# Making the weights' lower parts by an adding DMA instead of a subtraction

## The chip, the core and the metric

The kernel runs on one core of a Trainium2 chip. The metric is the time of one execution on the device, in microseconds; several executions are timed and their median is given. The core has five engines with instruction queues of their own: TensorE (PE in the profile; its weight loads are PEld), VectorE (DVE), ScalarE (ACT), GpSimd (POOL) and SyncE (SP), and 16 DMA engines that all queues share.

## What is computed

The reference is a decoder trunk of two layers on 512 tokens of 1024 features, in float32. Every layer has four sub-layers, each with a norm before and after it and a residual:

```python
for l in range(DEPTH):
    h = rmsnorm(x, ff1_pre_g[l])
    x = x + 0.5 * rmsnorm(swiglu(h, ff1_w1[l], ff1_w3[l], ff1_w2[l]), ff1_post_g[l])
    h = rmsnorm(x, mix_pre_g[l])
    y = token_mixer(h, ...)              # pooling, sparse attention and gMLP branches, gated and merged
    x = x + rmsnorm(y, mix_post_g[l])
    h = rmsnorm(x, mem_pre_g[l])
    y = memory_cross_attention(h, ...)   # 4 heads, into 256 memory tokens
    x = x + rmsnorm(y, mem_post_g[l])
    h = rmsnorm(x, ff2_pre_g[l])
    x = x + 0.5 * rmsnorm(swiglu(h, ff2_w1[l], ff2_w3[l], ff2_w2[l]), ff2_post_g[l])
```

## The kernel before

Products of float32 operands are made on TensorE in the format float32r, which holds fewer bits. So every operand is split into two parts, an upper part (the operand rounded to float32r) and a lower part (the operand less its upper part), and one product becomes three: upper times upper, upper times lower, lower times upper (`mm3`, line 439).

The weights come in blocks of 128 x 1024 values, 512 KB each, in the order of their use (`plan`). `Weights` (line 308) leads a block through three stations. `pump` issues its load on SP's queue into one of three raw buffers (`raw`, line 328). `parts` (line 348) splits it into one of four split buffers (`wh`, an upper and a lower half): ScalarE copies the raw block into the upper half (`act`, the instruction is at line 394), then `lo` has VectorE (line 398) or GpSimd (line 413) subtract the upper half from the raw block, whichever the planner takes to be done sooner, with the bonus `spare`. After that the raw buffer is free for a later load, which waits for it in SP's queue. `next` hands a block to the products (line 429), and `release` frees its split buffer after them. `ahead` says how many blocks ahead of the one in use may be split: 2, and 4 in the output products of a sub-layer. Some blocks aren't split (the compression's `cw1`, `wst`, `poolw`); they stay in a raw buffer until TensorE has used them.

There are 482 loads and 462 splits. A feed-forward layer has 66 blocks, of which 44 are used one after the other for 24 products of 512 columns each. Places in which the blocks' order differs:

- `first_blocks`: a sub-layer starts with four blocks on the first 256 tokens (24 products of 256 columns each), then, when the norm and transposition of the other tokens are done, the same four blocks on the other 256. Seven sub-layers start so behind another one.
- `token_out`: the output products of a sub-layer. Its last four blocks are used together, tile of tokens by tile of tokens (four tiles, six products of each block for a tile), so that the norm of the first tile can begin while the others are multiplied. There are eight of these. The next sub-layer's tokens are normed tile by tile by `chain` and `pre_norm` on VectorE, ScalarE and, for the power -1/2, GpSimd (line 468), then transposed on TensorE (line 437).
- The mixer's start: unsplit compression blocks (16 short products each) alternate with projection blocks.
- The cross-attention: 8 key blocks with 24 products of 256 columns, then 8 value blocks with 12 products of 512 columns, with the attention's own products between the later ones.

The program's order is made by a planner, `Clock`: a discrete estimate of when each engine is free and when each operand is ready, by which every helper (`act`, `tt`, `gtt`, ...) puts its instruction into the program. On the chip every engine runs its queue in that order and waits for semaphores.

Of the kernel before, what the change touches and what calls it, by code (L numbers as in the profile page):

```python
# [167 lines left out]
class Slots:  # L168
    """Buffers, each with the time from which it is free."""

# [18 lines left out]
    def retire(self, tiles):  # L189
        """These are given out no more."""  # L190
        self.gone = tiles
        self.free = [x for x in self.free if not any(x[2] is e for e in tiles)]
# [9 lines left out]
class Clock:  # L202
    """The order of the program: what the engines beside the tensor engine do is put into it where its operands are
    about ready, by an estimate of what every instruction takes."""

# [47 lines left out]
    def wait(self, when):  # L253
        """The main line's: time passes."""
        assert not self.inside
        while self.heap and self.heap[0][0] <= when:
            self.step()
        self.pe = self.now = max(self.pe, when)
# [10 lines left out]
    def reach(self, key):  # L269
        """The main line's wait for an event."""  # L270
        n = 0
        while key not in self.events:
            self.step()
            n += 1
            assert n < 100000, key
        self.wait(self.events[key])

    def after(self, *keys, margin=0.0):
        """A task's wait for events."""
        for key in keys:  # L280
            while key not in self.events:
                yield self.now + 0.2
            if self.events[key] + margin > self.now:
                yield self.events[key] + margin

    def take(self, slots, keep=0):
        """A task's wait for a buffer, of which `keep` others must be left."""
        while len(slots.free) <= keep or slots.first() > self.now:
            yield self.now + 0.2 if len(slots.free) <= keep else slots.first()
        return slots.pop()[2]  # L290

    def get(self, slots):
        """The main line's wait for a buffer."""
        n = 0
        while not slots.free:
            self.step()
            n += 1
            assert n < 100000
        when, _, t = slots.pop()
        self.wait(when)  # L300
        return t
# [6 lines left out]
class Weights:  # L308
    """The weights in the order of their use: loaded ahead, and split into two parts ahead."""

# [37 lines left out]
    def parts(self, k):  # L348
        b, n = self.b, k.cols
        raw, hi, lo = k.raw[:, :n], k.hl[:, 0, :n], k.hl[:, 1, :n]  # L350
        yield b.act(hi, raw, AF.Copy)
        r = b.lo(lo, raw, hi)
        self.raws.put(r, k.raw)
        k.raw = None
        k.ready = r
        self.pump()
# [28 lines left out]
class Builder:  # L385
    def __init__(self, tc, d, out):
        self.tc, self.nc, self.d, self.out = tc, tc.nc, d, out
        self.ck = Clock()
        self.spare = -0.5

    # Instructions, each with an estimate of the time at which its result is there.

# [22 lines left out]

    def lo(self, out, src, hi):
        """A block of weights' lower part, by whichever engine has it sooner."""
        ck = self.ck
        n = size(out)
        v = max(ck.free["v"], ck.now) + 0.07 + 0.00105 * n  # L420
        g = max(ck.free["g"], ck.now) + 0.1 + 0.0024 * n
        if g < v + self.spare:
            return self.gtt(out, src, hi.bitcast(F32), OP.subtract)
        return self.tt(out, src, hi.bitcast(F32), OP.subtract)

    def mm(self, out, w, x, first, last):
# [13 lines left out]
    def mm3(self, out, w, x, first, last):  # L440
        """out += w.T @ x for float32 operands given as their two exact parts."""
        (wh, wl), (xh, xl) = w, x
        self.mm(out, wh, xh, first, False)
        self.mm(out, wh, xl, False, False)
        self.mm(out, wl, xh, False, last)

    def split(self, hi, lo, src, scale=None, bias=None):
        """hi + lo = src, a tensor on chip, each with float32r's bits. To be run by a task; returns the time."""
        if scale is not None:
# [8 lines left out]
    def row(self, dst, src_row, n, eng=None):  # L458
        """A row of DRAM to every partition."""
        (eng or self.nc.gpsimd).dma_start(dst, bass.AP(tensor=src_row.tensor, offset=src_row.offset, ap=[[0, 128], [1, n]]))  # L460
        self.ck.op("g", 1.0)

    def rstd(self, out, ss, a, b):
        """out = (ss * a + b) ** -0.5. To be run by a task; returns the time."""
        n = out.shape[-1]
        v = self.small.tile([128, 4], F32, name="v", bufs=8)
        yield self.ts(v[:, :n], ss, float(a), float(b), OP.mult, OP.add)
        self.nc.gpsimd.tensor_tensor(out, v[:, :n], self.neghalf[:, :n], OP.pow)  # L468
        return self.ck.op("g", 0.46)
# [76 lines left out]
    def pre_norm(self, m, at, ng, left):  # L546
        """Normalises a tile of tokens from the sums of squares and transposes it, for sub-layer `at`."""
        ck = self.ck
# [28 lines left out]
    def proj(self, blk, bank, n0=0, n1=S):  # L577
        """bank[feature, token] = block.T @ h, over the whole of the contraction."""
        for k in range(KD):
# [10 lines left out]
    def first_blocks(self, keys):  # L590
        """The first products of a sub-layer, on the first half of the tokens while the others get ready."""
        ck = self.ck
# [7 lines left out]
        for m in (2, 3):  # L600
            ck.reach(("T", self.at, m))
        self.spare = -0.5
        for blk, bank in got:
# [4 lines left out]
    def token_out(self, l, ph, name, lhs, ready, nk, scale, tail):  # L608
        """y[token, :] = lhs.T @ w, its norm, the residual, and the next sub-layer's norm."""
        nc, ck, ws = self.nc, self.ck, self.ws  # L610
# [71 lines left out]
        blks = []  # L682
        self.spare = 4.0
        for m in range(NT):
# [48 lines left out]
    def gelu(self, out, z2, zh, t, scale):  # L733
        """out = zh (1 + tanh(c (z + a z^3))), with z2 = z^2, zh a multiple of z and the scale to match."""
        yield self.stt(t, z2, 1.0 / GA, zh, OP.add, OP.mult)
# [3 lines left out]
    def mixer(self, l, ph):  # L739
        tc, nc, d, ck = self.tc, self.nc, self.d, self.ck  # L740
        F, H, PS, ws, at = self.f, self.hl, self.ps, self.ws, self.at
        with tc.tile_pool(name=f"mix{l}", bufs=1) as pool, tc.tile_pool(name=f"mixs{l}", bufs=1) as few:
# [71 lines left out]

            # The keys, the queries and the compressed branch's tokens.
            KS = [ck.get(H), ck.get(H)]
# [18 lines left out]
            def blocks_of(s):  # L835
                """The overlapping blocks with their positions, two tokens to a column of partitions."""
                out = []
# [13 lines left out]
            def keys_evac(bank, i, dst, key):  # L851
                """Both halves of the partitions hold a group's keys."""
                r = 0.0
# [12 lines left out]
            def queries(c, bank):  # L866
                """Over the partitions: a head's upper and lower parts, in either order."""
                q = yield from ck.take(H)
# [20 lines left out]

            # The compression, beside the gMLP's projections.  # L890
            U, hid = [None] * 4, {}
# [14 lines left out]
            def hidden(s):  # L906
                """gelu of the hidden features, [feature, (half, group, block)], and the second product."""
                F.put(ck.now, *B[s])
# [51 lines left out]
            def gated_values(m, bank):  # L960
                """gelu and layer norm of a tile of tokens; doubling its input only scales the norm's epsilon."""
                yield from ck.after(("row", at, "gm"))
# [39 lines left out]

            self.spare = 2.5
            compress(1, 0)
# [45 lines left out]

            # The gMLP's products over the tokens.
            GM = [None] * 4
# [75 lines left out]
            def spatial():  # L1128
# [9 lines left out]
                F.put(ck.now, *VG, wst, rows["lng"], rows["lnb"], rows["gm"])  # L1138
                self.spare = -0.5

            tasks = self.attention(few, dict(KS=KS, KW=KW, V=V, VC=VC, Q=Q, gates=gates, msel=msel, mwin=mwin,
# [3 lines left out]

            # The pooling mixer.
            PL = [None] * 4
# [61 lines left out]
    def attention(self, few, o):  # L1209
        """The three branches of the sparse attention; returns its tasks."""  # L1210
        nc, ck = self.nc, self.ck
# [68 lines left out]
        def spreader():  # L1280
            """The probabilities of a block of keys, [key, token], in two parts."""
            for n in range(8):
# [55 lines left out]
        def output(n, bank):  # L1338
            """The values' two parts lie in the two halves of the partitions."""
            c, g = divmod(n, 2)  # L1340
# [234 lines left out]
```

## Time and profile before

| what | value |
|---|---|
| median of 3 runs | 2781.05 us (2778.61 to 2781.05) |
| span of the profiled execution | 2778.1 us |
| TensorE busy | 2728.2 us (98%) |
| VectorE busy | 1418.9 us (51%) |
| ScalarE busy | 1038.0 us (37%) |
| GpSimd busy | 324.3 us (12%) |
| DMA moved | 270.45 MB, mean 97 GB/s |
| TensorE's granted clock, mean | 0.996 |

The profiled execution is another one than the timed ones; its span runs from its first to its last instruction and lies 2.95 us under the median. In a row of the timeline the columns are the start and the duration in us, the engine, the line in the kernel, the operation, the tiles written and read (buffer numbers left out) and their shape, how many instructions the row merges, and in brackets the engine's idle time before the row and what ended it. In a row of a group the columns are line, engine, operation, tiles, shape, count, and then busy time in us and mean ns of one, idle time before them, and what ended most of it.

### The profile page before, as it was taken

The page shows a single profiled execution, that of the slowest core. Times are in us where ns is not written, and L with a number is a line of the kernel's source. Part 1 is how long each engine was busy: PE and PEld are TensorE (multiplying, and loading weights), DVE is VectorE, ACT ScalarE, POOL GpSimd, SP SyncE. Part 2 cuts the span into 40 slices and gives each one's busy share as a digit, 9 for nine tenths or more (in the row PEclk, how much of TensorE's full clock was granted, in tenths as well). Part 3 has the DMA queues.
Part 4 walks back from the last instruction along what each step waited for, and adds up shares of the span by engine and source line. Part 5 has one row for each costly group of instructions (what it writes and reads, how often), then busy time and mean ns, then how long its engine had stood idle before and what let it go on. Part 6 is the DMA issues. An engine that isn't in the chain of part 4 may idle for free.

```text
span 2778.1 us, 34462 instructions
## 1 busy us (share of the span) xinstructions
PE 2728.2 (98%) x13624; PEld 2303.3 (83%) x13624; DVE 1418.9 (51%) x2536; ACT 1038.0 (37%) x1894; POOL 324.3 (12%) x299
## 2 busy tenths in 40 slices
PE   8999999999999999999999999999999999999998
PEld 7888888887888888888888888888778898888887
DVE  4443254889536554442354432639885465544422
ACT  3222234456435443222232222445564354432221
POOL 0000020411222020000010000213112220200000
PEclk9999999999999999999999999999999999999999
DMA  4232224311234323332233322342122343233322
GB/s 144 94 112 98 99 89 125 101 58 61 84 114 123 113 77 99 114 99 97 78 99 105 107 93 97 88 135 87 54 69 84 106 143 104 70 101 107 99 93 74
DMA packets 77970, 270.45 MB, mean 97 GB/s; under 512 B 10160, under 2 KB 10672, under 8 KB 77808
## 3 DMA queue, kind: packets, MB, share of 16 engines
q1 hardware_dynamic: 71568, 255.56, 28.6%
q0 software_dynamic: 3136, 10.25, 1.4%
q10 hardware_dynamic: 3104, 2.45, 0.3%
q8 instruction: 106, 1.74, 0.3%
q14 instruction: 56, 0.46, 0.0%
HBM read 266.12 MB, written 2.10 MB: 97 GB/s over the span
## 4 chain that ended last, share of the span: by engine, by line
PE 89%; DVE 8%; ACT 1%; issue 1%; DMA 0%; POOL 0%; ACTq 0%; SPq 0%; DVEq 0%; POOLq 0%
PE ps L429 86%; PE ps L437 2%; DVE x L402 2%; DVE hl L398 1%; DVE wh L398 1%; DVE f L407 1%; DVE ast L398 1%; ACT junk L394 1%; DVE f L1224 0%; DVE f L402 0%; DVE f L398 0%; DVE mf L1224 0%; DVE mf L407 0%; DVE sty L398 0%; DMA raw<-in_ff_w_dram 0%
## 5 line engine op out<-in xcount | busy, mean ns | idle before, releaser
L429 PE MATMUL ps<-hh,wh 128*128 128x512 f32 (+1 forms) x4864 | 1402.5, 370 | 1.8 <-ACT hh L394 1.4
L429 PEld LDWEIGHTS ps<-hh,wh 128*128 128x128 f32 x4864 | 886.6, 190 | 149.4 <-ACT hh L394 1.8
L429 PE MATMUL ps<-hlo,wh 128*128 128x512 f32 (+1 forms) x2432 | 899.6, 370 | 0.1
L398 DVE TENSOR_TENSOR wh<-raw,wh 128x1024 fp32r<-128x1024 f32 x402 | 505.9, 1261 | 604.6 <-ACT wh L394 604.1
L394 ACT ACTIVATE wh<-raw 128x1024 fp32r<-128x1024 f32 x462 | 485.1, 1052 | 729.6 <-PE ps L429 437.0
L429 PEld LDWEIGHTS ps<-hlo,wh 128*128 128x128 f32 x2432 | 462.3, 190 | 72.5 <-DVE v L409 0.4
L429 PE MATMUL ps<-wh,hl 128*128 128x512 f32 x2016 | 469.4, 391 | 0.0
L429 PEld LDWEIGHTS ps<-wh,hl 128*128 128x128 f32 x2016 | 376.9, 188 | 77.6
L413 POOL TENSOR_TENSOR wh<-raw,wh 128x1024 fp32r<-128x1024 f32 (+2 forms) x60 | 147.3, 2458 | 1285.9 <-ACT wh L394 1285.9
L398 DVE TENSOR_TENSOR f<-ps,f 128x512 f32<-128x512 f32 (+1 forms) x169 | 116.7, 691 | 318.6 <-PE ps L429 211.3
L429 PE MATMUL ps<-wh,g 128*128 128x512 f32 x960 | 228.1, 396 | 0.0
L429 PEld LDWEIGHTS ps<-wh,g 128*128 128x128 f32 x960 | 179.3, 188 | 42.6
L429 PE MATMUL ps<-hl,wh 128*128 128x512 f32 (+1 forms) x960 | 195.1, 351 | 0.0
L429 PEld LDWEIGHTS ps<-hl,wh 128*128 128x128 f32 x960 | 152.4, 190 | 20.4
L394 ACT ACTIVATE hl<-f 128x512 fp32r<-128x512 f32 (+1 forms) x75 | 47.3, 630 | 252.7 <-DVE f L398 213.1
L437 PE MATMUL ps<-ident,f 128*128 128x128 f32 (+1 forms) x573 | 102.3, 289 | 32.4 <-DVE f L402 29.9
L394 ACT ACTIVATE hl<-ps 128x512 fp32r<-128x512 f32 (+2 forms) x180 | 80.4, 468 | 103.1 <-PE ps L429 82.5
L398 DVE TENSOR_TENSOR hl<-ps,hl 128x512 fp32r<-128x512 f32 (+2 forms) x180 | 91.9, 529 | 44.0 <-ACT hl L394 42.7
L437 PEld LDWEIGHTS ps<-ident,f 128*128 128x128 f32 (+1 forms) x573 | 71.8, 145 | 47.7 <-DVE f L402 35.5
L402 DVE SCALAR_TENSOR_TENSOR f<-f,ps 128x512 f32<-128x512 f32 x120 | 81.8, 682 | 46.5 <-PE ps L429 42.1
L394 ACT ACTIVATE g<-f 128x512 fp32r<-128x512 f32 x40 | 25.3, 633 | 181.3 <-DVE f L398 181.3
L402 DVE SCALAR_TENSOR_TENSOR x<-f,sty,x 128x512 f32<-128x512 f32 x64 | 78.5, 1267 | 10.2 <-POOL sty L468 10.2
(186 smaller groups left out, 1991.7 us busy)
## 6 DMA issues: line engine op xcount, KB each, us to landing
raw<-in_ff_w_dram SPq DMA_DIRECT2D x264, 512.0 KB, 3.5
raw<-in_wf_dram SPq DMA_DIRECT2D x80, 512.0 KB, 3.5
raw<-in_cw_dram SPq DMA_DIRECT2D x16, 512.0 KB, 3.6
raw<-in_wmo_dram SPq DMA_DIRECT2D x16, 512.0 KB, 3.6
raw<-in_wq_dram SPq DMA_DIRECT2D x16, 512.0 KB, 4.2
raw<-in_wk_dram SPq DMA_DIRECT2D x16, 512.0 KB, 3.8
raw<-in_wv_dram SPq DMA_DIRECT2D x16, 512.0 KB, 3.8
raw<-in_wo_dram SPq DMA_DIRECT2D x16, 512.0 KB, 3.7
```

Of the source, the lines that this page charges most:

```text
L394: self.nc.scalar.activation(out, src, func, accum_out=accum_out, **kw)
L398: self.nc.vector.tensor_tensor(out, a, b, op)
L402: self.nc.vector.scalar_tensor_tensor(out, a, s, b, op0, op1)
L407: self.nc.vector.tensor_scalar(out, a, s0, None, op0=op0)
L413: self.nc.gpsimd.tensor_tensor(out, a, b, op)
L429: self.nc.tensor.matmul(out, w, x, start=first, stop=last)
L437: self.nc.tensor.transpose(out, src, self.ident)
```

## The change

`parts` writes the upper half as before; a second ScalarE pass over the same raw block, with the scale -1, writes the negated upper part into the lower half; then a DMA issued from GpSimd's queue adds the raw block onto the lower half. The raw buffer is free, and the split block ready, when that DMA has landed. The planner is told 1.0 us of GpSimd's time for the issue, and readiness 4.15 us after it. `lo` and the settings of `spare` go, so neither VectorE nor GpSimd subtracts for the weights. The splitting of tensors made on the chip (`split`) stays as it was. Other lines of the diff only take out comments and docstrings.

```diff
     def parts(self, k):
         b, n = self.b, k.cols
         raw, hi, lo = k.raw[:, :n], k.hl[:, 0, :n], k.hl[:, 1, :n]
-        yield b.act(hi, raw, AF.Copy)
-        r = b.lo(lo, raw, hi)
+        b.act(hi, raw, AF.Copy)
+        yield b.act(lo, raw, AF.Copy, scale=-1.0)
+        b.nc.gpsimd.dma_start(lo, raw, accum_op=OP.add)
+        r = b.ck.op("g", 1.0) + 4.0
         self.raws.put(r, k.raw)
         k.raw = None
         k.ready = r
...
-    def lo(self, out, src, hi):
-        """A block of weights' lower part, by whichever engine has it sooner."""
-        ck = self.ck
-        n = size(out)
-        v = max(ck.free["v"], ck.now) + 0.07 + 0.00105 * n
-        g = max(ck.free["g"], ck.now) + 0.1 + 0.0024 * n
-        if g < v + self.spare:
-            return self.gtt(out, src, hi.bitcast(F32), OP.subtract)
-        return self.tt(out, src, hi.bitcast(F32), OP.subtract)
```

## Rows read from the trace of the kernel before

**Rows 1.** The profile's head: the span, and TensorE's busy time with its weight loads.
```profile
span 2778.1 us, 34462 instructions
...
PE 2728.2 (98%) x13624; PEld 2303.3 (83%) x13624; DVE 1418.9 (51%) x2536; ACT 1038.0 (37%) x1894; POOL 324.3 (12%) x299
```

**Rows 2.** The costliest groups of instructions: those that split the weights.
```profile
L398 DVE TENSOR_TENSOR wh<-raw,wh 128x1024 fp32r<-128x1024 f32 x402 | 505.9, 1261 | 604.6 <-ACT wh L394 604.1
L394 ACT ACTIVATE wh<-raw 128x1024 fp32r<-128x1024 f32 x462 | 485.1, 1052 | 729.6 <-PE ps L429 437.0
...
L413 POOL TENSOR_TENSOR wh<-raw,wh 128x1024 fp32r<-128x1024 f32 (+2 forms) x60 | 147.3, 2458 | 1285.9 <-ACT wh L394 1285.9
```

**Rows 3.** The timeline around a sub-layer's start: VectorE, ScalarE, TensorE.
```profile
1377.88 1.41 DVE L402 SCALAR_TENSOR_TENSOR x<-f,sty,x 128x512 f32<-128x512 f32 x2 [0.67 <-POOL sty L468]
...
1394.09 5.33 DVE L402 SCALAR_TENSOR_TENSOR x<-f,sty,x 128x512 f32<-128x512 f32 x2
...
1389.23 1.07 ACT L394 ACTIVATE wh<-raw 128x1024 fp32r<-128x1024 f32 x1 [1.57 <-PE ps L429]
...
1394.93 1.05 ACT L394 ACTIVATE wh<-raw 128x1024 fp32r<-128x1024 f32 x1
...
1394.08 0.28 PE L429 MATMUL ps<-hh,wh 128*128 128x256 f32 x1
...
1405.23 1.12 PE L437 MATMUL ps<-ident,f 128*128 128x128 f32 x4 [2.73 <-DVE f L402]
```

**Rows 4.** The timeline in an even stage: a block's ScalarE pass, its first products.
```profile
193.72 1.06 ACT L394 ACTIVATE wh<-raw 128x1024 fp32r<-128x1024 f32 x1 [2.95 <-issue]
...
209.79 0.62 PE L429 MATMUL ps<-hh,wh 128*128 128x512 f32 x2
```

**Rows 5.** The groups of GpSimd by line: its DMA issues.
```profile
L460 POOL DMA_DIRECT2D f<-in_gains_dram x30 | 16.6, 555 | 554.1 <-DVE hl L398 487.5 <-DVE g L398 30.3 <-issue 21.2
```

**Rows 6.** DMA: SP's queue; issues (KB of one, median us to landing).
```profile
q1 hardware_dynamic: 71568, 255.56, 28.6%
...
raw<-in_ff_w_dram SPq DMA_DIRECT2D x264, 512.0 KB, 3.5
...
f<-in_gains_dram POOLq DMA_DIRECT2D x30, 256.0 KB, 4.0
...
out_dram<-x SPq DMA_DIRECT2D x8, 256.0 KB, 2.1
...
raw<-in_wst_dram SPq DMA_DIRECT2D x2, 256.0 KB, 2.6
```

**Rows 7.** The timeline at a sub-layer's last blocks: ScalarE, TensorE.
```profile
1369.93 1.06 ACT L394 ACTIVATE wh<-raw 128x1024 fp32r<-128x1024 f32 x1 [4.54 <-PE ps L429]
...
1369.03 5.76 PE L429 MATMUL ps<-wh,g 128*128 128x512 f32 x24
```

**Rows 8.** The timeline at the mixer's start: ScalarE, SP's queue, TensorE's compression products.
```profile
428.94 1.06 ACT L394 ACTIVATE wh<-raw 128x1024 fp32r<-128x1024 f32 x1
...
441.83 1.06 ACT L394 ACTIVATE wh<-raw 128x1024 fp32r<-128x1024 f32 x1
...
438.05 0.33 SPq L328 DMA_DIRECT2D raw<-in_wf_dram  x1
...
437.19 1.89 PE L429 MATMUL ps<-f,raw 128*128 128x64 f32 x16
444.47 1.89 PE L429 MATMUL ps<-f,raw 128*128 128x64 f32 x16
```

**Rows 9.** The timeline in the cross-attention: ScalarE, SP's queue, TensorE's key products.
```profile
885.33 1.05 ACT L394 ACTIVATE wh<-raw 128x1024 fp32r<-128x1024 f32 x1
...
893.42 1.06 ACT L394 ACTIVATE wh<-raw 128x1024 fp32r<-128x1024 f32 x1 [1.26 <-PE ps L429]
...
887.67 0.33 SPq L328 DMA_DIRECT2D raw<-in_wk_dram  x1
...
890.41 12.76 PE L429 MATMUL ps<-hl,wh 128*128 128x256 f32 x105
```

More of the change, by code (lines that the diff above doesn't have):

```diff
@@ L388, in __init__ @@
         self.ck = Clock()
-        self.spare = -0.5
     def act(self, out, src, func, accum_out=None, **kw):
@@ L601, in first_blocks @@
             ck.reach(("T", self.at, m))
-        self.spare = -0.5
         for blk, bank in got:
@@ L682, in token_out @@
         blks = []
-        self.spare = 4.0
         for m in range(NT):
@@ L1001, in by_token @@
                 ws.release(blk)
-            self.spare = 2.5
             compress(1, 0)
@@ L1138, in spatial @@
                 F.put(ck.now, *VG, wst, rows["lng"], rows["lnb"], rows["gm"])
-                self.spare = -0.5
             tasks = self.attention(few, dict(KS=KS, KW=KW, V=V, VC=VC, Q=Q, gates=gates, msel=msel, mwin=mwin,
```

## The prediction

> **What bounds the kernel now.** I read the page's busy times first. TensorE is busy for 2728.2 of 2778.1 us [rows 1], so all other engines together can give back at most the 49.9 us in which it idles, and some of that is the first load and the last store. The work that the change touches is large but lies beside TensorE: 402 subtractions of 1.26 us on VectorE, 60 of 2.46 us on GpSimd, and 462 ScalarE passes of 1.05 us that make the upper parts [rows 2]. So the share of busy time says nothing about this change. What counts is how early each weight block is ready before TensorE turns to it, and this I read from the timelines, stage by stage: an even stage, the last blocks of a sub-layer, the first blocks of the next, and two stages in which blocks are short or share their buffers.
>
> **The change, part by part.** *Removed:* 505.9 us of VectorE and 147.3 us of GpSimd [rows 2]. None of it is on the path in the even stages. It is on the path in one way: while GpSimd subtracts, VectorE's operations with two operands on chip are slow. At a sub-layer's start a pair of them took 5.33 us, against 1.41 us for the same pair without it, and TensorE then idled 2.73 us for the tokens' chain [rows 3]. Without the subtraction that chain is 3.9 us earlier, so this idle time goes. There are seven such starts.
>
> *Added to ScalarE:* 462 passes of 1.05 us, 485 us, which makes about 1523 us of busy time. In the even stage a block's first pass starts at 193.72 and TensorE reaches the block at 210.0 [rows 4], 16.3 us later. That lead hides the second pass; if the lead were gone, the whole 485 us would be bare.
>
> *Added to GpSimd's queue:* 462 DMA issues. Its present ones take 0.56 us each [rows 5]: 257 us, so GpSimd goes from 324 to some 434 us. Each issue waits for the second pass, and behind it in the same queue wait the small powers of the norms and the merges' additions.
>
> *Added latency, the term that decides.* Call L the time from the end of the second pass to the moment at which TensorE sees the sum. No row shows an adding DMA. The nearest are: GpSimd's own loads of 256 KB, 4.0 us from issue to landing; SP's loads, 2.6 us for 256 KB and 3.5 for 512 KB, so 0.9 us for each further 256 KB [rows 6]. A plain copy of 512 KB from GpSimd's queue would then be 4.9 us. The sum also has to read its destination, up to 1.8 us more: 6.7. I take the middle, L = 5.8 us; the lower end is SP's 3.5 us. From below, GpSimd's path would have to be as quick as SP's; from above I have no row, since an adder's own rate stands nowhere. The Trainium skill (Collectives: The Full Stack, "The bandwidth ceiling: the fold count and why AG ≠ RS ≠ AR") says that adding in a DMA costs no cycles of its own but halves the rate because two sources are read. By that rule L is the 6.7 us just named and the sum below would be 25 us higher; no row here can show it.
>
> A block's preparation takes 1.06 + 1.24 = 2.3 us before the change where VectorE subtracts, or 3.5 us where GpSimd does; it becomes 2.1 + L = 7.9 us. Where is the lead smaller than that?
>
> 1. The even stages, most of the 462 blocks: lead 16.3 us [rows 4]. Nothing is lost.
>
> 2. The last blocks of a sub-layer, eight times. Only four buffers hold split blocks, and the last four blocks are used together, so the last one's preparation begins when the block before these four is let go. ScalarE starts at 1369.93. TensorE has 3 x 6 products ahead of it, at 0.233 us each (24 in 5.76 us) [rows 7]: 4.2 us, so it needs the block at about 1373.9. After the change it is ready at 1369.93 + 2.12 + L = 1372.05 + L. Lost: L - 1.85 = 3.95 us; 8 x 3.95 = 32 us.
>
> 3. The first blocks of the next sub-layer, seven times. The first pass starts at 1389.23 and TensorE reaches the block at 1394.08 [rows 3]: 1389.23 + 2.12 + L is 3.1 us late. The third block's pass starts at 1394.93, now 1.05 later behind the second block's second pass: ready at 1398.1 + L = 1403.9, while its turn, two half-blocks of 2.9 us (worked out in point 5) after the first, is 1399.8 + 3.1: 1.0 us more. From these 4.1 us goes the idle 2.73 us, which would have come right after. Net 1.4 us; 7 x 1.4 = 10 us.
>
> 4. The mixer's start, twice. Unsplit blocks (the compression's) share the three raw buffers with split ones, one of each to a step. A pass starts at 428.94; TensorE reaches this block at 431.6, which is the 437.19 of the next unsplit block less 5.6 for the block's own products [rows 8]. After the change it is ready at 436.9: 5 us lost. From then on the ring of raw buffers sets the pace. In the kernel before, a load follows the subtraction that frees its buffer (438.05, with ScalarE at 441.83 [rows 8]). With the buffer held for 7.9 us, the unsplit blocks' buffers, let go by TensorE, come free first, and two steps take a load (3.7), two passes (2.1), L, one block's products (5.6) and one unsplit block (1.7): 13.1 + L = 18.9, or 9.4 us a step. Before it is 7.3 (437.19 to 444.47 [rows 8]). Seven steps x 2.1 = 15 us. Together 20, for both layers 40 us. Bounds: 19 us with L = 3.5; 79 us if the ring stays as it is, with one buffer for all split blocks (3.7 + 2.1 + L = 11.6 a step).
>
> 5. The cross-attention's keys and values, 16 blocks a layer, of 2.9 us each (24 products; 105 take 12.76 us [rows 9]). The pass at 885.33 and its subtraction free the buffer for the load at 887.67, whose block's pass is at 893.42 [rows 9]. After the change three buffers go round in 3.7 + 2.1 + L = 11.6 us, 3.9 us a block: 1.0 short. Attention products stand between the later blocks and give the ring time, so I take 6 us a layer, 12 in all; bounds 0 and 31.
>
> 6. VectorE's relief in the attention: at most a few short idle stretches of TensorE; I take 5 us back.
>
> Sum: 32 + 10 + 40 + 12 - 5 = 89 us, and 28 us for each us of L (8 from point 2, 7 from 3, 9 from 4, 4 from 5). The profiled span is 2778.1 us; it becomes 2867. The median of the runs is 2781.05, 2.95 above the span. Forecast: 2870 us, 3.2% slower.
>
> **The rivals.** *A short transfer.* If L is 3.5 us, as SP's loads of the same size [rows 6], point 2 gives 13, point 3 gives -6 (the idle time goes and less comes), point 4 gives 19, point 5 some 2, less 5: +23 us, 2804. For it: source and destination are both on chip. Against: GpSimd's 256 KB already take 4.0. The Trainium skill (DMA: Bandwidth & Descriptors, "Anatomy of one DMA — SWDGE (gpsimd) path") fits 2.0 us plus the bytes at 436 GB/s, 3.2 us for this block, which would make it 2796; by the same fit 256 KB take 2.6 us, and the 4.0 of the row speaks against it.
>
> *Faster.* The mechanism is the freed chain at the seven starts. It decides if L is below 2.6 us, where all losses together equal the 2.7 us x 7 + 5 that come back. The nearest row is a 256 KB store by SP, 2.1 us [rows 6]: point 2 gives 2, point 3 -16, point 4 7, less 5: -12 us, 2769. Against it: no load of that size or queue is as short.
>
> *GpSimd's queue.* An issue that waits for ScalarE holds up the powers behind it, which the tokens' chain needs. At a start two issues could each hold one for two passes, 2.1 us: the idle 2.73 us stays and 4.2 us minus what is late anyway come on top, about 4 us x 7: 2898. For it: queues run in order. Against: the planner puts an issue where ScalarE is about done.
>
> *DMA engines as the bound.* SP's queue holds 28.6% [rows 6] of the span for 482 loads, 1.65 us each. There are 6.0 us of span for a block. If the sum alone holds the engines for more than 4.3 us a block, they set the pace everywhere: with 5 us, 482 x 1.65 + 462 x 5 = 3105. Against: two reads of 512 KB at the loads' rate are 3.3 us.
>
> **How the numbers follow.** Forecast 0.66, with a range of its own from L = 4.4 (2831) to L = 8 (2932). Short transfer 0.11, faster or the same 0.09 (faster 0.05, same 0.04), GpSimd's queue 0.08, DMA-bound 0.06. The range leaves out the last and the faster case: 2792 to 2965. About 0.2%, 5.6 us, can be told from no change. Slower by more: 0.66 + 0.11 + 0.08 + 0.06 = 0.91.
>
> **What will show it.** L itself, from the adding DMA's row (issue to landing): 5.8. TensorE's waits for that DMA: near 4 us once before each sub-layer's last products, near 3 and 1 at the first blocks, and a row of them in the compression stage and among the keys. The pair of VectorE operations at the starts back near 1.4 us. TensorE's busy time about unchanged, its idle time about 139 us. The forecast is wrong if L lies outside 4.4 to 8, if the loss is spread over the even stages (then the DMA engines are the bound), or if GpSimd's powers come late.

## The result, and the profile after

The changed kernel takes 2948.51 us (2944.92 to 2952.97) against 2781.05: a ratio of 1.0614, with a 95% interval of 1.0601 to 1.0627. The sign and the range were right, the size was not: 2870 was forecast, and the change costs 6.1% where 3.2% stood.

The page of the changed kernel (head and busy times; DMA queues with packets, MB, share of 16 engines; the two groups that make the weights' parts; issues with KB and median us to landing):

```profile
span 2942.9 us, 35541 instructions
...
PE 2780.7 (94%) x13624; PEld 2333.2 (79%) x13624; DVE 864.6 (29%) x2134; ACT 1467.1 (50%) x2356; POOL 553.1 (19%) x701
...
q0 software_dynamic: 69664, 251.65, 46.9%
q1 hardware_dynamic: 71568, 255.56, 25.7%
...
L395 ACT ACTIVATE wh<-raw 128x1024 fp32r<-128x1024 f32 (+2 forms) x924 | 920.6, 1046 | 722.4 <-PE ps L420 432.9
...
L353 POOL DMA_DIRECT2D wh<-raw x462 | 399.1, 865 | 1931.0 <-ACT wh L395 1594.8
...
wh<-raw POOLq DMA_DIRECT2D x456, 512.0 KB, 5.5
raw<-in_ff_w_dram SPq DMA_DIRECT2D x264, 512.0 KB, 4.6
```

The two subtraction groups [rows 2] are gone and VectorE has fallen by 554 us, but it bounded nothing. TensorE's idle time (span less busy) rose from 49.9 us [rows 1] to 162.2, by 112. Its busy time rose too, from 2728.2 to 2780.7, by 52.5 us with the same 13624 products: the same work ran more slowly. The two make up the 164.8 us of span. Loads take 4.6 us where they took 3.5 [rows 6], since the sum keeps the same 16 engines busy for 46.9% of the span.

TensorE's waits say for whom it idles (us in total, times, longest). The changed kernel:

```profile
PE ps L420 <- DMA wh<-raw: 111.7, 53, 4.8
PE ps L428 <- DVE f L403: 27.6, 13, 7.5
```

Before, the first line did not exist, and the second, the wait for the tokens' chain, was:

```profile
PE ps L437 <- DVE f L402: 29.9, 15, 7.6
```

So the new wait is for the sum. Of the old one the part at the seven starts has gone from 17.6 to 12.5 us; the rest lies ahead of the kernel's first product, where a wait of 3.7 us is new.

Where? The windows view of four stages (us, busy time of each engine, PEclk the granted clock, DMA share, GB/s). Before: an even stage, the compression, keys and values, a sub-layer's end:

```profile
47.00:264.00 217.00, 217.00 (x959) 179.78 (x958) 89.30 (x101) 62.08 (x79) 2.32 (x4) 1.00 0.32 104
438.90:506.90 68.00, 67.14 (x390) 58.65 (x390) 27.80 (x40) 27.42 (x50) 15.75 (x7) 1.00 0.48 146
890.40:948.30 57.90, 57.90 (x378) 53.05 (x377) 36.26 (x52) 29.16 (x48) 0.00 (x0) 1.00 0.47 142
1369.70:1394.10 24.40, 24.37 (x114) 19.52 (x113) 12.39 (x26) 10.20 (x21) 7.97 (x8) 1.00 0.09 25
```

After, the same stages, and then 6 us right behind the wait in the last of them:

```profile
50.00:267.00 217.00, 217.00 (x960) 179.74 (x959) 41.41 (x60) 101.26 (x121) 37.49 (x45) 1.00 0.85 200
455.50:550.00 94.50, 77.95 (x390) 65.55 (x390) 21.45 (x44) 36.78 (x60) 11.40 (x14) 0.87 0.57 151
945.40:1022.10 76.70, 63.75 (x377) 56.67 (x376) 16.07 (x35) 42.04 (x62) 13.10 (x16) 0.93 0.92 215
1449.30:1480.90 31.60, 27.15 (x113) 21.54 (x112) 11.35 (x25) 12.32 (x23) 4.51 (x7) 0.89 0.33 81
...
1458.00:1464.00 6.00, 5.68 (x13) 4.46 (x14) 1.65 (x5) 0.69 (x2) 0.56 (x1) 0.50 0.26 87
```

Three readings. The even stage has not moved: 217.0 busy of 217.0 us, with the DMA engines at 0.85. The other three are longer, and in each the granted clock is below 1: after a wait TensorE runs at 0.50, that is 1.2 GHz. And among the keys and values the DMA engines are at 0.92.

The same done for every stage of both traces, from the first product of one stage to that of the next; the third column is the added idle time, the fourth the added half of the time that TensorE spent at half clock:

| stage | later, us | idle | clock | forecast |
|---|---|---|---|---|
| before the first product | 4.1 | 2.5 | 0 | none |
| even stages, outputs up to their last blocks | 0.6 | 0 | 0 | 0 |
| sub-layers' ends, 8 | 47.1 | 33.7 | 11.5 | 32 |
| starts, 8 | 17.8 | 15.2 | 5.1 | 10 |
| mixer's start and compression, 2 | 60.9 | 38.5 | 22.1 | 40 |
| keys and values, 2 | 39.9 | 26.6 | 11.9 | 12 |
| branches, 2 | -5.5 | -4.4 | 0 | -5 |

### The profile page after: what moved, and what is told of

The parts are those of the page before. It is cut to its first block, busy times and chain, and to the rows that moved or that the text cites. A ratio compares the mean times of both kernels' runs of the same rounds, so it can differ in the third digit from the quotient of the medians.

```text
span 2942.9 us, 35541 instructions
## 1 busy us (share of the span) xinstructions
PE 2780.7 (94%) x13624; PEld 2333.2 (79%) x13624; DVE 864.6 (29%) x2134; ACT 1467.1 (50%) x2356; POOL 553.1 (19%) x701
## 3 DMA queue, kind: packets, MB, share of 16 engines
q0 software_dynamic: 69664, 251.65, 46.9%
q1 hardware_dynamic: 71568, 255.56, 25.7%
## 4 chain that ended last, share of the span: by engine, by line
PE 74%; DMA 12%; issue 6%; DVE 4%; ACT 3%; POOL 1%; ACTq 0%; POOLq 0%; SPq 0%; DVEq 0%
PE ps L420 73%; DMA wh<-raw 7%; ACT wh L395 2%; PE ps L428 2%; DMA raw<-in_wt_dram 1%; DMA raw<-in_wv_dram 1%; DVE hl L399 1%; DMA raw<-in_wf_dram 1%; DMA raw<-in_wk_dram 1%; ACT junk L395 1%; DVE f L403 0%; DVE ast L399 0%; DVE f L408 0%; DVE f L1211 0%; DMA x<-in_x_dram 0%
## 5 line engine op out<-in xcount | busy, mean ns | idle before, releaser
L395 ACT ACTIVATE wh<-raw 128x1024 fp32r<-128x1024 f32 (+2 forms) x924 | 920.6, 1046 | 722.4 <-PE ps L420 432.9
L353 POOL DMA_DIRECT2D wh<-raw x462 | 399.1, 865 | 1931.0 <-ACT wh L395 1594.8
L420 PE MATMUL ps<-wh,hl 128*128 128x512 f32 x2016 | 482.3, 397 | 22.9 <-DMA wh<-raw 22.7
L399 DVE TENSOR_TENSOR f<-ps,f 128x512 f32<-128x512 f32 (+1 forms) x158 | 109.2, 691 | 676.4 <-ACT junk L395 499.7
L420 PE MATMUL ps<-wh,g 128*128 128x512 f32 x960 | 235.6, 404 | 13.4 <-DMA wh<-raw 13.4
L420 PE MATMUL ps<-wh,hh 128*128 128x512 f32 (+1 forms) x256 | 77.3, 387 | 17.7 <-DMA wh<-raw 17.7
L395 ACT ACTIVATE junk<-ps 128x512 bf16<-128x512 f32 x64 | 37.9, 592 | 95.6 <-PE ps L420 85.1
```

Source lines behind the costliest of these rows:

```text
L353: b.nc.gpsimd.dma_start(lo, raw, accum_op=OP.add)
L395: self.nc.scalar.activation(out, src, func, accum_out=accum_out, **kw)
L399: self.nc.vector.tensor_tensor(out, a, b, op)
L420: self.nc.tensor.matmul(out, w, x, start=first, stop=last)
```

## The experiments

The theory: a block costs time only where its preparation, longer by L and a pass, exceeds its lead; in these places L is the price. Its rivals: the DMA engines' share, the second ScalarE pass, the planner's order, GpSimd's queue. A delay is given against the kernel before in the same series. The first four kernels were timed once each, against one execution of the kernel before, 2783.8 us, which is the longest on record; the others took 2773.7 to 2783.2. By the profiled spans, against 2778.1 us, the four delays are about 4 us larger, and the comparisons between the four stay the same.

**A shorter sum.** The added block is cut to 512, then to 64 of 1024 columns, which leaves the remaining columns of the lower part at the negated upper part; all instructions and waits stay.

```diff
-        b.nc.gpsimd.dma_start(lo, raw, accum_op=OP.add)
+        b.nc.gpsimd.dma_start(lo[:, :n // 2], raw[:, :n // 2], accum_op=OP.add)
```

> The adding DMA covers the first 512 of the 1024 columns only; the other half of each lower part stays the negated upper part, so that part of the sum is left out. Latency theory (the loss stands where a block's lead is shorter than its preparation, and the clock falls after each such wait): the latency of the sum falls from 5.8 to about 4.4 us, TensorE's waits for it from 112 to about 65 us, and the time from 2948 to about 2870 us. Rival, ScalarE: the second pass and its place in ScalarE's queue are the cost; the time stays within 15 us of 2948.

> The adding DMA covers 64 of the 1024 columns only; the rest of each lower part stays the negated upper part, so that part of the sum is left out. Latency theory: the latency falls to some 3.3 us, which only the last blocks and the compression stage still feel, and the time to about 2810 us. Rival, ScalarE's second pass: within 15 us of 2948. Rival, GpSimd's queue (an issue that waits holds what is behind it): the number of issues is the same, so the time stays above 2900.

Measured: 2861.99 and 2809.68, against 2783.8: 78.2 and 25.9 us. The DMA's rows, of the half and of the 64 columns:

```profile
wh<-raw POOLq DMA_DIRECT2D x456, 256.0 KB, 3.8
```

```profile
wh<-raw POOLq DMA_DIRECT2D x462, 32.0 KB, 2.2
```

With 0.3 us from the pass's end to the issue, L is 2.5, 4.1 and, in full, 5.8 us, and the delay 25.9, 78.2 and 167.5 us. L carries most of the price: 33 us for each us between the first two, and 53 between the last two, where 28 was forecast. So something is added as the transfer grows; the copy and the ring show what. The 64-column run has all 462 passes and all 462 issues: neither the second pass nor GpSimd's queue can be the main cost, since either would have kept the time near 2948 or above 2900.

**A plain copy.** The same bytes without the addition, so that the lower part is the raw block.

```diff
-        b.nc.gpsimd.dma_start(lo, raw, accum_op=OP.add)
+        b.nc.gpsimd.dma_start(lo, raw)
```

> The same DMA of the same size without the addition: the lower part becomes a copy of the raw block, so the sum is left out. If the second read of the sum is what makes it long, the latency falls from 5.8 to the 4.9 us that I worked out for a plain copy, GpSimd's queue's share of the DMA engines from 46.9% to about half, and the time to about 2900 us. If a sum costs what a copy costs, latency and time stay (2948, within 15).

Measured: 2846.68, 62.9 us, much less than expected. The page of the copy:

```profile
q0 software_dynamic: 69664, 251.65, 25.1%
...
L353 POOL DMA_DIRECT2D wh<-raw x462 | 248.6, 538 | 1986.2 <-ACT wh L395 1800.9
...
wh<-raw POOLq DMA_DIRECT2D x456, 512.0 KB, 3.6
raw<-in_ff_w_dram SPq DMA_DIRECT2D x264, 512.0 KB, 3.5
```

For the same 251.65 MB the addition raises the engines' share from 25.1 to 46.9%, the latency from 3.6 to 5.5 us and GpSimd's issue from 0.54 to 0.86. Loads beside copies take 3.5 us as before, beside sums 4.6. The addition is the larger part of the loss, some 100 of 167.5 us.

**The second pass alone.** The kernel before, with the negation by ScalarE as in the change, but the sum by VectorE and GpSimd under the old rule; no DMA adds.

```diff
-        yield b.act(hi, raw, AF.Copy)
-        r = b.lo(lo, raw, hi)
+        b.act(hi, raw, AF.Copy)
+        yield b.act(lo, raw, AF.Copy, scale=-1.0)
+        r = b.lo(lo, raw, lo)
...
-            return self.gtt(out, src, hi.bitcast(F32), OP.subtract)
-        return self.tt(out, src, hi.bitcast(F32), OP.subtract)
+            return self.gtt(out, src, hi.bitcast(F32), OP.add)
+        return self.tt(out, src, hi.bitcast(F32), OP.add)
```

> The second ScalarE pass stays, but VectorE or GpSimd adds the raw block onto it, as the planner chose in the kernel before: the pass without the DMA. Latency theory: preparation is 3.4 us on VectorE and 4.5 on GpSimd, about 1 us more than before the change: some 20 us, about 2800. Rival, ScalarE's second pass is the cost: above 2900.

Measured: 2823.02, 39.2 us, more than expected. In the trace 27.1 lie at the starts, 14.8 in the compression, 4.5 at the ends and 2.8 ahead of the first product; the branches give back 6.2. At the starts ScalarE also takes the tokens' squares and makes the upper parts of their transposes. TensorE waits there, twice at each of the seven, for the lower parts that VectorE makes of them:

```profile
PE ps L430 <- DVE hlo L399: 22.3, 14, 3.3
```

So the pass is not free where ScalarE is on the tokens' chain. I had priced it only as a part of a block's preparation. But the 27.1 us are not the pass's alone: GpSimd still adds beside VectorE here, and in the 64-column run, which has the pass and neither engine's additions, the starts are only 6.2 us late.

**Products in the place of the wait.** At each of the eight ends 17 products into a spare bank stand before the last block's first ones.

```diff
+                if m == 0 and i == tail - 1 and self.ps.free:
+                    spare = min(self.ps.free, key=lambda x: x[:2])[2]
+                    for _ in range(17):
+                        nc.tensor.matmul(spare, lhs(0, 0)[0], blks[0].hl[:, 0, :512], start=True, stop=True)
```

> The changed kernel with 17 idle products (into a free bank that nobody reads) put on TensorE ahead of the last block's products at the eight sub-layer ends, where TensorE waits some 4 us for the sum. They take about the 4 us of the wait. Clock theory (the fall of the granted clock after a wait comes from TensorE's idleness): TensorE's waits there vanish, the half-clock stretches after them vanish too (seven in the changed kernel's record, some 11 us lost), and the time falls by about 10 us, to 2938. Rival, the clock falls for another reason (the DMA traffic, the sum of activity): the half-clock stretches stay and the time does too, or rises where a wait was shorter than 4 us.

Measured: 2950.22, ratio 1.0619 [1.0592, 1.0647]: no gain that shows; the two executions lie 14 us apart, so a gain of a few us would not. At the seven ends inside the kernel the time lost to half clock went from 10.2 us to none, so it does come from the idle time. The end of [rows 7] in this run, products and what follows them:

```profile
1456.00:1476.00 20.00, 19.76 (x88) 15.24 (x87) 5.47 (x13) 5.44 (x12) 1.98 (x3) 1.00 0.45 110
```

But the total stayed: the products take some 4 us at every end, where the wait had been 1.3 to 4.8, so that the ends gained only 3.4 us. There the terms nearly add up: 31 us of products for 24 of idle time and 12 of half clock. In this execution, the slower of the two, the starts lost 4.4, the keys and values 5.8, and the branches gave back 5.4 less; why is not shown. So the half clock at the ends is real and costs what the granted clock says; that it would be a gain of the whole kernel is not shown.

**More raw buffers.** Two more in the cross-attention, one more at the mixer's start, for which two of eight tiles of the mixer are given up.

```diff
-            extra = [pool.tile([128, 528], F32, name=f"mf{i}") for i in range(8)]
+            extra = [pool.tile([128, 528], F32, name=f"mf{i}") for i in range(6)]
+            more = [pool.tile([128, 1024], F32, name=f"rawm{i}") for i in range(1)]
+            ws.raws.put(ck.now, *more)
...
+            more = [pool.tile([128, 1024], F32, name=f"rawm{i}") for i in range(2)]
+            ws.raws.put(ck.now, *more)
```

> The changed kernel with more raw buffers where I hold their ring for the cause: two more in the cross-attention, one more in the mixer up to its branches (there two of the mixer's eight extra working tiles are given up for the room). Ring theory: the 40 us lost among keys and values go almost wholly, the 54 us of the compression stage fall to about half; about 2885 in all, the ends and starts of sub-layers as they were. Rival, the DMA engines' rate sets the pace there (they are busy 73% of the span): both stages keep their losses, 2948.

Measured: 2901.85, ratio 1.0445 [1.0424, 1.0466]: 47 us come back. The compression is 9.0 us later than before in place of 53.8: the ring was its cause. (The branches lose 23.7 of it again, probably for the two tiles; no run gave up the tiles alone.) Keys and values are still 17.4 us late. Their windows, with the ring enlarged, the two layers:

```profile
933.80:1000.80 67.00, 60.22 (x377) 53.13 (x376) 16.03 (x35) 42.79 (x62) 12.48 (x15) 1.00 0.98 250
2370.30:2436.40 66.10, 59.81 (x377) 53.10 (x376) 16.02 (x35) 42.61 (x62) 12.44 (x15) 1.00 0.99 251
```

The clock is at 1.00 and the DMA engines are at 0.98 and 0.99: what remains here is their bound. The page says why. A sum holds them for 46.9% of 2942.9 us over 462, 3.0 us, a load for 25.7% over 482, 1.6: together 4.6 us a block. TensorE needs a block here every 57.9 / 16 = 3.6 us; in the even stage above it needed 40 blocks in 217.0 us, one every 5.4, and 4.6 of 5.4 is the share of 0.85 seen there.

**The negation on VectorE.**

```diff
-        b.act(hi, raw, AF.Copy)
-        yield b.act(lo, raw, AF.Copy, scale=-1.0)
+        yield b.act(hi, raw, AF.Copy)
+        yield b.ts(lo, hi.bitcast(F32), -1.0)
```

> The changed kernel with the negated upper part written by VectorE from the upper part, not by a second ScalarE pass; the adding DMA as it is. Queue theory (the second pass delays the tokens' chain in ScalarE's queue at the sub-layers' starts, as the run with the pass and no DMA showed with 27 us there): the starts lose some 10 us less, the ends a little, 2930 to 2940. Rival, the latency of the sum is all: the same within 5 us, since VectorE's operation takes 0.7 us for 1.05. A second rival: VectorE's operation keeps GpSimd from issuing, so that the latency grows and the time with it, above 2950.

Measured: 2971.51, ratio 1.0696 [1.0677, 1.0715], worse than the change; my expectation failed. The pass itself is shorter, 0.7 us against 1.05, but starts are 36.0 us late (17.8) and ends 54.7 (47.1). The timeline at a sub-layer's end shows its place in the queue:

```profile
2344.63 1.06 ACT L395 ACTIVATE wh<-raw 128x1024 fp32r<-128x1024 f32 x1 [1.83 <-PE ps L420]
...
2346.29 2.85 DVE L399 TENSOR_TENSOR f<-ps,f 128x512 f32<-128x512 f32 x4 [2.77 <-ACT junk L395]
...
2349.06 0.68 DVE L408 TENSOR_SCALAR wh<-wh 128x1024 fp32r<-128x1024 f32 x1
2350.04 0.86 POOL L353 DMA_DIRECT2D wh<-raw  x1 [5.37 <-DVE wh L408]
```

The upper part is there at 2345.7, the negation starts 3.4 us later, behind four multiplications of the outputs by the norm's gain. Two engines ahead of the DMA are two queues to stand in. The second rival, a GpSimd that VectorE keeps from issuing, is not borne out: the sum's median from issue to landing is 5.5 us and its issue 0.86, as in the change.

**The DMA only where leads are long.** The kernel before, with the DMA first in the mixer's branch blocks alone, then also in the gated layers' even blocks; all other blocks are subtracted as before.

```diff
+        key = k.key
...
-        yield b.act(hi, raw, AF.Copy)
-        r = b.lo(lo, raw, hi)
+        if key[1] in ("brg", "brp", "brn") or key[1] == "f" and key[2] > 17:
+            b.act(hi, raw, AF.Copy)
+            yield b.act(lo, raw, AF.Copy, scale=-1.0)
+            b.nc.gpsimd.dma_start(lo, raw, accum_op=OP.add)
+            r = b.ck.op("g", 1.0) + 4.0
+        else:
+            yield b.act(hi, raw, AF.Copy)
+            r = b.lo(lo, raw, hi)
```

The second run's condition:

```diff
+        if (key[2] in ("w1", "w3") and key[3] > 3 or key[2] == "w2" and (key[3], key[4]) < (1, 5)) or (key[1] in ("brg", "brp", "brn") or key[1] == "f" and key[2] > 17):
```

> The kernel before with the adding DMA only for the blocks of the mixer's three branches (where attention keeps VectorE busy and leads are long); all other blocks are subtracted as before. Latency theory: no block there is late, and VectorE's relief gives back the 5 to 7 us that this stage gained in every run so far: about 2775, some 0.2% faster than before. Rival, the DMA has a price of its own wherever it is used: 2790 or more.

> The kernel before, with the negated pass and the adding DMA only for the blocks that TensorE reaches long after their preparation begins: the gated layers' blocks from the third pair on (w1 and w3 from index 4, w2 up to the fifth of its second half) and the mixer's branch blocks; all blocks at starts and ends, in the compression and in the keys and values are subtracted as before. If a block's lead alone decides, the DMA costs nothing here: 2779 us, within 6 us, with no wait of TensorE for it. If the DMA also costs where leads are long (engines that it shares with the loads, ScalarE's second pass, the order of GpSimd's queue), the time is above 2790. By the chain theory there is no gain either, since GpSimd still subtracts at the starts.

Measured: ratios of 1.0002 [0.9993, 1.0010] and 0.9997 [0.9987, 1.0006]. The page of the second:

```profile
q0 software_dynamic: 42880, 154.97, 30.6%
...
L356 POOL DMA_DIRECT2D wh<-raw x276 | 239.5, 868 | 1182.2 <-ACT wh L402 1008.8
...
wh<-raw POOLq DMA_DIRECT2D x276, 512.0 KB, 5.5
```

276 of the 462 sums, each as long as in the change, cost nothing; TensorE never waits for one. The whole loss belongs to the other 186 blocks. Nothing is gained either: the 5 us and more that VectorE's relief was to give back in the branches did not come.

**The planner's order.** Its estimate of the sum is cut from 5 us to 1.3.

```diff
-        r = b.ck.op("g", 1.0) + 4.0
+        r = b.ck.op("g", 0.3) + 1.0
```

> The changed kernel with another estimate in the planner: the sum ready 1.0 us after an issue of 0.3 us, in place of 4.0 after 1.0. This moves where the waiting instructions and the loads are put in the queues, and nothing of what they do. If buffers and the transfer set the time, it stays within 20 us of 2948. If the order of the queues that follows from the planner's 5 us is the cause of a part of the 165 us, it falls to 2920 or less.

Measured: 2978.49, ratio 1.0717 [1.0684, 1.0750], 30 us later than the change, spread over branches (10.8), keys and values (7.0), starts (4.7). So the order does matter, but that the planner's estimate is too long is not what costs the time; a shorter one costs more. A longer one, nearer to the 5.8 us measured, was not run: how much of the 165 us a better order would save stays open.

**The freed chain without the DMA.** One number of the kernel before: GpSimd gets no subtraction from a sub-layer's last blocks to the next one's first. Then the same, from the moment at which the last four blocks are ready.

```diff
-        self.spare = 4.0
+        self.spare = -20.0
```

```diff
                 if m == 1:
                     ws.ahead = 2
+                    self.spare = -20.0
```

> The kernel before with one number changed: from a sub-layer's last blocks to its successor's first ones all subtractions go to VectorE (spare -20 in place of 4), none to GpSimd; no DMA adds. If GpSimd's subtractions are what slows VectorE's pairs there, the pair at the starts takes 1.41 us in place of 5.33; three subtractions of 1.26 us are added to VectorE's queue in the same time. The freed chain then brings 3.9 less about 2.5 at seven starts: 10 us, or 2771, with the idle 2.73 us shorter. Rival: the subtractions stand in the chain in VectorE's own queue and take what the pair gives back: 2779 within 6, or later.

> The kernel before, GpSimd barred from subtracting only once a sub-layer's last four blocks are ready (spare 4 for those blocks as before, -20 from there to the next sub-layer's first blocks); no DMA adds. The run with GpSimd barred at the ends too gained 22.5 us at the starts and lost 7.2 us at the ends, where TensorE waited up to 1.4 us for VectorE's subtraction. If these are separate effects, the 7.2 us come back: 2765 less 7, or 2758, and the starts keep their gain. Rival: the gain at the starts depends on the blocks at the ends having been moved too (VectorE's queue is then shifted), and it stays near 2765.

Measured: 2765.04, ratio 0.9950 [0.9935, 0.9965], then 2757.70, ratio 0.9927 [0.9913, 0.9940]: 0.5 and 0.7% faster than the kernel before, by more than the noise. VectorE at a start of the second one, and TensorE's waits:

```profile
1387.38 1.23 DVE L398 TENSOR_TENSOR wh<-raw,wh 128x1024 fp32r<-128x1024 f32 x1
1388.88 1.23 DVE L398 TENSOR_TENSOR wh<-raw,wh 128x1024 fp32r<-128x1024 f32 x1
1390.03 1.41 DVE L402 SCALAR_TENSOR_TENSOR x<-f,sty,x 128x512 f32<-128x512 f32 x2
```

```profile
PE ps L437 <- DVE f L402: 16.7, 13, 8.0
```

The pair takes 1.41 us where it took 5.33 [rows 3], the wait for the chain is 16.7 us in place of 29.9. The starts come 22.7 us earlier, in the first of the two kernels 22.5, of which 13.6 are idle time and 8.5 half clock. So the mechanism that I had counted on was real, and worth more than its idle time.

## Why the prediction was right, and where it was short

**L: right in size, by luck in part.** 5.5 us from issue to landing and 0.3 before it are the 5.8 forecast. But the working had 4.9 us for a plain copy and up to 1.8 more for the second read, and took the middle. The copy took 3.6, and the addition 1.9 more, the whole of the second read: what was too long in the one part made up for what the middle took off the other and for the 0.3 us ahead of the issue. The Trainium skill (Collectives: The Full Stack, "The bandwidth ceiling: the fold count and why AG ≠ RS ≠ AR") says that adding is free in itself but that reading two sources halves the rate. The trace agrees on the rate: a sum holds the engines for 3.0 us (46.9% of 2942.9 over 462), a copy for 1.5 (25.1% of 2844.6), 1.93 times as long. By the fit in the Trainium skill (DMA: Bandwidth & Descriptors, "Anatomy of one DMA — SWDGE (gpsimd) path") the copy is estimated at 3.2 us. It took 3.6, and the sum, at 5.5, is outside that fit.

**Point 1: right.** The even stages have not moved, and the runs with long leads show the same for 276 blocks.

**Point 2, first part: the idle time is right, 33.7 against 32,** and the wait is the one that was named. The timeline of the end that goes with rows 7 and of the start behind it (start, us, engine):

```profile
1449.52 2.01 ACT L395 ACTIVATE wh<-raw 128x1024 fp32r<-128x1024 f32 x2 [3.59 <-PE ps L420]
...
1451.82 0.87 POOL L353 DMA_DIRECT2D wh<-raw  x1 [4.71 <-ACT wh L395]
1458.32 10.76 PE L420 MATMUL ps<-wh,g 128*128 128x512 f32 x33 [4.45 <-DMA wh<-raw]
...
1482.92 0.50 PE L420 MATMUL ps<-hh,wh 128*128 128x256 f32 x2 [1.60 <-DMA wh<-raw]
...
1483.49 1.99 ACT L395 ACTIVATE wh<-raw 128x1024 fp32r<-128x1024 f32 x2
...
1484.40 1.41 DVE L403 SCALAR_TENSOR_TENSOR x<-f,sty,x 128x512 f32<-128x512 f32 x2 [0.75 <-POOL sty L459]
...
1485.39 0.61 ACT L395 ACTIVATE junk<-x 128x512 bf16<-128x512 f32 x1
...
1487.55 0.66 PE L428 MATMUL ps<-ident,f 128*128 128x128 f32 x4 [1.61 <-DVE f L403]
```

The passes end at 1451.5, TensorE goes on at 1458.3. L here is 6.8 us and not the median: over the eight ends it is 4.9 to 9.4, in the mean 6.5, longest at the mixer's own two. With 6.5 the sum would have been 8 x 4.7 = 37, so that the 32 came so near is luck in part too. With half the bytes it is 3.7 to 5.9.

**Point 2, second part: the half clock.** What is missing at the ends, 15 us, is mostly the 11.5 us of half clock behind their waits: there the last products run at 0.50, and the next sub-layer's first ones come later by it. That such waits bring it could have been read before the change, at the very idle time that I meant to remove. The kernel before, behind the 2.73 us of rows 3:

```profile
1404.80:1408.20 3.40, 2.96 (x14) 2.97 (x15) 2.45 (x6) 1.23 (x4) 0.55 (x1) 0.50 0.46 154
```

Before, 5 of 8 waits of over 2 us were followed by half clock, after, 21 of 30. I priced waits by their length alone, and **"TensorE's busy time about unchanged" is wrong**: 51 of the 52.5 us are half clock. By this reading only the part at ends and starts, 16.6 us, can have lengthened the path; the other 34 lie in the two stages of the next points, where ring and engines set the pace.

**Point 5: mis-sized, 39.9 us where 12 stood; the largest miss.** I took the ring of raw buffers as the only limit and looked for the DMA engines' bound as an average over the kernel, 6.0 us a block, in a rival that I gave 0.06. In this stage a block has 3.6 us and needs 4.6 of the engines. The rival was right in one stage, as the share of 0.92 shows, and 0.98 with the ring out of the way and the clock at 1.00. Of the 39.9 us more buffers gave back 22.5; 17.4 are the engines' bound.

**Point 4: mis-sized, 60.9 us where 40 stood.** The timeline of the compression shows the bound that I had put at the far end, one buffer for all split blocks:

```profile
479.49 2.00 ACT L395 ACTIVATE wh<-raw 128x1024 fp32r<-128x1024 f32 x2 [5.83 <-DMA raw<-in_wf_dram]
...
486.32 0.33 SPq L328 DMA_DIRECT2D raw<-in_wt_dram  x1
486.74 0.38 SPq L328 DMA_DIRECT2D raw<-in_cw_dram  x1
490.08 2.01 ACT L395 ACTIVATE wh<-raw 128x1024 fp32r<-128x1024 f32 x2 [3.58 <-DMA raw<-in_wt_dram]
...
496.92 0.80 PE L420 MATMUL ps<-wh,hh 128*128 128x512 f32 x1 [0.56 <-DMA wh<-raw]
496.93 0.33 SPq L328 DMA_DIRECT2D raw<-in_wt_dram  x1
...
500.30 2.00 ACT L395 ACTIVATE wh<-raw 128x1024 fp32r<-128x1024 f32 x2 [3.02 <-DMA raw<-in_wt_dram]
```

Load at 486.3, passes at 490.1, landing and the next load at 496.9: 10.6 us a step, with no product of TensorE in it, against 9.4 forecast and 7.3 before [rows 8]. Seven steps are 23 us, with 3.5 at the stage's start 27 of the 30 us a layer. The half clock here lies within the ring's time. The run with another buffer confirms the ring: 53.8 us of compression became 9.0.

**Point 3: the freed chain came only in part,** 17.8 us where 10 stood. VectorE's pair is back at 1.41 us, as forecast. But the next squares of the tokens (1485.39) stand behind two passes of 1.99 us (1483.49) on ScalarE, and TensorE still waits 1.61 us for the chain, after 1.60 for the first block's sum, for which 3.1 stood. At this start, for which 1.4 us stood, the sum of it all is 0.3. Nearly all of the 17.8 lies at four others, those of the mixer and the cross-attention, 4.0 to 4.8 us each: there TensorE also waits up to 2.2 us for VectorE's operations on the tokens and runs at half clock behind these waits. Why at these four is open.

**Left out:** the 4.1 us before TensorE's first product. The kernel's first block has L in front of it too: its sum lands at 19.2 us, where the first product had started at 16.8. The rest are eight transposes that wait for the tokens' chain and now stand ahead of that product, which starts at 21.0.

**Point 6: right in size, 5.5 against 5; VectorE's relief as its reason is not borne out.** The run with the second pass alone, in which VectorE subtracts as much as before (1408 us busy against 1419), gives back 6.2 us in the same stage, and the run with the DMA in the branches alone only 2. What gives the time back there is open.

Together: keys and values 28 us more than forecast, compression 21, ends 15, starts 8, first block 4: the 76 us by which 89 fell short of 165.

**The rivals.** *Short transfer* and *faster* needed an L that isn't there. *GpSimd's queue* did not hold up the powers, though an issue took 0.86 us where 0.56 stood. In the changed kernel GpSimd sat idle before every one of the 64 (`sty` and `st`) until VectorE had written its operand (us in total, times, longest):

```profile
POOL sty L459 <- DVE v L410: 139.0, 32, 12.4
POOL st L459 <- DVE v L410: 76.3, 32, 6.3
```

What stays open: how much of the 16.6 us of half clock at ends and starts would return at full clock. Products at the ends, too many at some of them, took the half clock away there and brought nothing in total.

## What to carry to other kernels

In this kernel moving work to a DMA cost its latency wherever a block's lead was shorter than its new preparation, and nothing where it was longer: read the lead stage by stage, and the DMA engines' budget per block stage by stage too. Price a wait of TensorE by its length and, where nothing else sets the pace behind it, by the half-clock time that the trace shows behind such waits. Ahead of relieving an engine that has time to spare, look for the few places where it is late: here the planner's setting for those gave 0.5 to 0.7%, where moving all of its subtractions cost 6.1%.

## What the runs showed of the hardware

An adding DMA of 512 KB from on-chip memory to on-chip memory took 5.5 us where the copy took 3.6, held the engines 1.93 times as long, and slowed the loads beside it from 3.5 to 4.6 us. GpSimd took 0.86 us to issue it, against 0.54 for the copy. An addition of 256 KB took 3.8 us, one of 32 KB 2.2. After 21 of 30 waits of over 2 us TensorE ran at half its clock, for 3.4 to 10.2 us; with products in the place of the wait, at the ends, the clock stayed up. A pair of VectorE's operations took 5.33 us while GpSimd subtracted and 1.41 where it was barred from it.
